# Queries and keys by half a Strassen product, and attention in one order written by hand

## The chip, the cores and the metric

The kernel runs on one core of a Trainium2 chip. The metric is the device time in microseconds (us) of one execution, the median of several. The engines of a core are TensorE (PE; PEld are its weight loads), VectorE (DVE), ScalarE (ACT) and GpSimd (POOL); SyncE (SP) issues the DMAs. Each engine takes its instructions in the order in which they stand in its own list, and waits there for the semaphores of others. Matmuls write PSUM banks of 128 x 512 float32; everything else lives in SBUF.

## The reference

Two layers on x of 1024 rows and 1024 columns: dilated attention, then a state-space layer (S5). The change touches the attention:

```python
proj = h @ w_in                       # h: 1024 x 1024
n_qkv = 3 * N_GROUPS_A * ATTN_WIDTH   # 3 groups, 16 heads of 64
qkv = proj[..., :n_qkv].reshape(B, S, 3, N_GROUPS_A, ATTN_HEADS, HEAD_DIM)
z = proj[..., n_qkv:]
for g, (window, dilation) in enumerate(((128, 1), (512, 4), (2048, 16))):
    o, l = dilated_group_attention(qkv[:, :, 0, g], qkv[:, :, 1, g], qkv[:, :, 2, g],
                                   rel_bias, window, dilation)
    ...
wts = jax.nn.softmax(jnp.stack(lses), axis=0)
o = jnp.sum(wts[..., None] * jnp.stack(outs), axis=0)
return (o * jax.nn.silu(z)) @ w_out
```

Inside a group each query meets up to 128 + 1 keys at steps of the dilation: logits with a bias, softmax, and a weighted sum of values. The three groups' outputs are merged by their log-sum-exps, gated, and projected out.

## The kernel before

All large products are done in fp32r with a high and a low part of each operand and three products: high x high, low x high, high x low. `split` makes the parts: ACT casts the high part (L88, for queries with a factor at L91), and DVE, or POOL for the attention's weights, subtracts it from the source (L89, L92).

The stages follow one another: norm and transposition of x to h (two row halves th of 512, kept as hh and hl), the values of all heads by Strassen-Winograd products (class Quads, L431), which leaves seven sums of h in SBUF; then the attention; then its gates and out-projection (`attn_gate`, L115 again and L966), then layer 1.

The attention runs over 8 pairs of heads and 3 groups: 24 units. A unit loads and splits a 1024 x 128 weight of queries, makes the two row halves of the queries in a PSUM bank each (`proj_half` and `proj_part`, L115: 8 blocks of the contraction x 3 products = 24 matmuls of 128x512 a bank), and `evac_q` splits a bank into qh and ql in the group's own order of rows. The same is done for the keys (`evac_k`: kh and kl). Then, for each of two halves u of the query tiles (`attn_unit`): logits into psl (L530), bias and running maximum on DVE (L536), the negated maxima nm (L542), exponentials on ACT (L547), transposes into pt (L558), their split to ph, and value products into pso (L607, or L633 for the last group), copied and added to O (L617, L618, L638). `put_ms` sends maxima and sums through DRAM (transpose ptm, L645). When a pair is complete, `merge_weights` computes the three groups' weights, and POOL multiplies each O by its weights mw, loaded back from DRAM (L748), and adds them up (L750). Between these, POOL also makes rotation tables for layer 1 (L1397 to L1402).

Two banks (psj) hold projections, two pairs of banks psl hold logits, two each are for pt and pso; q and k tiles have two buffers each, lg and ph three. The order on each engine is the Tile scheduler's: the program is written unit by unit, with projections' loads and splits and the logits put ahead by `high_priority(AHEAD)`. It thereby mixes a unit's projections with the transposes and value products of the units before. After the last pair the gates (8 heads' pairs x 2 row halves x 24 matmuls, L115) mix with the end of the attention in the same way; the last pair's merged O, its gate and its split gh are what the last part of the out-projection needs.

Of the kernel before, what the change touches and what calls it, by code (L numbers as in the profile page):

```python
# [52 lines left out]

class Ctx:
# [40 lines left out]
def load_w(c, src):  # L95

    nc = c.nc
    with c.tc.high_priority(AHEAD):
        raw = c.wraw.tile([P, KT * P], F32, tag="wraw", name="wraw")
        nc.sync.dma_start(raw, src)  # L100
        hi = c.wsp.tile([P, KT * P], F32R, tag="whi", name="whi")
        lo = c.wsp.tile([P, KT * P], F32R, tag="wlo", name="wlo")
        c.last_lo = split(c, hi, lo, raw, engine=c.w_engine).ins
    return hi, lo
# [147 lines left out]
def evac_k(c, ps, g, t0, k):  # L252

    n = ps.shape[1] // ORD[g]
    at = t0 // ORD[g]
    hi, lo = (t.rearrange("p (r l) -> p r l", r=ORD[g])[:, :, at:at + n] for t in k)
    split(c, hi, lo, ps.rearrange("p (l r) -> p r l", r=ORD[g]))


# [42 lines left out]
class Quads:  # L302
# [4 lines left out]
    def __init__(self, c):  # L307
# [8 lines left out]
        def tt(o, x, y, op):  # L316
            nc.vector.tensor_tensor(o, x, y, op=op)

        def parts(slots, t):
            hi, lo = (c.vslot(s, F32R) for s in slots)  # L320
            split(c, hi, lo, t)
            return hi, lo
# [19 lines left out]
        self.rows = [a11, a12, s4, a22, s1, s2, s3]  # L342
# [7 lines left out]
    def quad(self, raw, order, product, banks, use):  # L350
# [12 lines left out]
        def weights(i):  # L363
            with c.tc.high_priority(AHEAD):
# [13 lines left out]
                hi, lo = (c.wsp.tile([P, KT * P], F32R, tag=t, name=t)[:, 0:4 * n].rearrange("p (k x) -> p k x", k=4)  # L378
# [103 lines left out]
def load_v(c, p, g):  # L482


    nc = c.nc
    vp = c.attn.tile([P, KT, P], F32, tag="vp", name="vp", bufs=1)
    o = ORD[g]
    off = c.v_dr.offset + (g * 2 + p // 4) * S * H + p % 4 * P

    for dst, at, step in (((vp, 0, P),), ((vp[:, 0::2], 0, 1), (vp[:, 1::2], o * P, 1)), ((vp, 0, 1),))[g]:  # L490
        src = bass.AP(c.v_dr.tensor, off + at * H, [[o * H, P], [step * H, dst.shape[1]], [1, P]])
        nc.sync.dma_start(dst, src)
    vs = c.attn.tile([P, KT, 2, P], F32R, tag="vs", name="vs", bufs=1)
    if g == 2:
        split(c, vs[:, :, 0], vs[:, :, 1], vp)
    else:
        split(c, vs[:, :, :, 0:64], vs[:, :, :, 64:128], vp.rearrange("p b (h d) -> p b h d", h=2))
    return vs


# [3 lines left out]


def attn_unit(c, g, u, q, k, v, bt, ms, O):


    nc = c.nc
    qh, ql = q  # L510
    kh, kl = k
    lg = c.attn.tile([P, 2, 4, 256], F32, tag="lg", name="lg", bufs=3)
    tiles = []
    for js in ((0, 1, 2, 3),) if g == 2 else ((0, 1), (2, 3)):

        psl = c.psa.tile([P, 2, H], F32, tag="psl", name="psl")
        parts, at = [], 0
        for j in js:
            qt = u * 4 + j
            m = (7 - qt, 1 - qt % 2, 0)[g]  # L520
            start = (max(m - 1, 0) * P, qt // 2 * 256, qt * P)[g]
            w = 256 if m else 128
            tiles.append(w)
            parts.append((j, slice(at, at + w), slice(qt * P, qt * P + P), slice(start, start + w)))
            at += w
        with c.tc.high_priority(AHEAD):
            for j, o, qs, ks in parts:
                for n, (x, y) in enumerate(((qh, kl), (ql, kh), (qh, kh))):
                    for h in range(2):
                        nc.tensor.matmul(psl[:, h, o], x[HEADS[h], qs], y[HEADS[h], ks],  # L530
                                         start=j == js[0] and n == 0, stop=n == 2, skip_group_check=True)
        for j, o, _, _ in parts:
            w = tiles[j]
            for h in range(2):
                col = ms_col(g, 0, h, u * 4 + j)
                nc.vector.tensor_tensor_reduce(  # L536
                    lg[:, h, j, 0:w], psl[:, h, o], bt[:, h, 256 - w:256], scale=1.0, scalar=-3.0e38,
                    op0=ALU.add, op1=ALU.max, accum_out=ms[:, col:col + 1])
    nm = c.small.tile([P, 2, 4], F32, tag="nm", name="nm")
    at = (4 - 4 * u, 4 * u, 4 * u)[g]  # L540
    mx = ms[:, 0:16].rearrange("p (h t) -> p h t", h=2)[:, :, at:at + 4]
    nc.vector.tensor_scalar(nm, mx, -1.0, None, op0=ALU.mult)  # L542
    for h in range(2):
        for j, w in enumerate(tiles):
            col = ms_col(g, 1, h, u * 4 + j)
            b = (3 - j, j ^ 1, j)[g]
            nc.scalar.activation(lg[:, h, j, 0:w], lg[:, h, j, 0:w], AF.Exp, bias=nm[:, h, b:b + 1],  # L547
                                 accum_out=ms[:, col:col + 1])
    (pv_last if g == 2 else pv_first)(c, g, u, lg, v, O)
    if u == 1:  # L550
        put_ms(c, g, ms)


def transposed(c, lg, blocks, name):

    pt = c.pst.tile([P, H], F32, tag="pst", name=name)
    for n, (h, j, part) in enumerate(blocks):
        c.nc.tensor.transpose(pt[:, n * P:(n + 1) * P], lg[:, h, j, part * P:part * P + P], c.ident)  # L558
    return pt


def split_weights(c, pt, wd):
    t = c.attn.tile([P, 2, H], F32R, tag="ph", name="ph", bufs=3)
    hi, lo = t[:, 0], t[:, 1]
    split(c, hi[:, 0:wd], lo[:, 0:wd], pt[:, 0:wd])
    return hi, lo
# [12 lines left out]
def pv_first(c, g, u, lg, vs, O):  # L579


    nc = c.nc

    if g == 0:
        first = [(6 - 4 * u - j, j, [(j, 0), (j + 1, 1 if j < 2 or u == 0 else 0)]) for j in range(3)]
        single = [(7 - 4 * u, 0, [(0, 1)])]
        if u == 0:
            single.append((3, 3, [(3, 0)]))
        banks = [first[:2], first[2:] + single]
    else:  # L590
        banks = [[(4 * u + j, j, [(j, 0), (j + 1, 0)]) for j in (0, 2)],
                 [(4 * u + 1 + j, j, [(j, 1)]) for j in (0, 2)]]
    for h in range(2):
        po = c.pso.tile([P, H], F32, tag="pso", name="pso")
        jobs = []
        for bank in banks:
            blocks = [(h, j, part) for _, _, parts in bank for j, part in parts]
            wd = P * len(blocks)
            hi, lo = split_weights(c, transposed(c, lg, blocks, "pt"), wd)
            at = 0  # L600
            for kb, col, parts in bank:
                n = P * len(parts)
                for x in (hi, lo):
                    jobs.append((po[:, col * P:col * P + n], vs[:, kb, h], x[:, at:at + n]))
                at += n
        for n, (o, l, r) in enumerate(jobs):
            nc.tensor.matmul(o, l, r, start=n == 0, stop=n == len(jobs) - 1, skip_group_check=True)  # L607
        out = out_tile(c, g, O)

        rows = HEADS[h]  # L610
# [6 lines left out]
        nc.scalar.copy(dst, fr[0])  # L617
        nc.vector.tensor_tensor(dst, dst, fr[1], op=ALU.add)  # L618


def pv_last(c, g, u, lg, vs, O):


# [78 lines left out]
def attn_pair(c, p, w_in, h):  # L702
# [3 lines left out]
    for g in range(3):  # L706
# [17 lines left out]
        if g == 1:  # L724
            run_merge(c)
# [1061 lines left out]
```

## Time and profile before

| what | us |
|---|---|
| median of 3 runs | 1662.56 (1661.94 to 1662.82) |
| span of the profiled execution | 1660.9 |
| the attention's eight pairs | about 332 to 1097 in the span |
| PE / DVE / ACT / POOL busy in the span | 1640.8 / 1025.7 / 710.2 / 460.7 |

Only the span of the profiled execution is known of it; it lies 1.7 us below the median of the runs. Rows of grouped instructions give the line, engine, operation, output <- inputs, shapes, count, then busy time and mean ns of one, then the engine's idle time before them and what ended it. Rows of windows give for each engine the busy time in a stretch and (after x) the instructions, then PE's granted clock, the share of DMA time and GB/s. Rows of the chain of waits give start, length and what ran.

### The profile page before, as it was taken

Reading aid. Unit: us, or ns where it says so; the run is one execution under the profiler, and the core shown is the slowest. Engines: PE = TensorE matmul, PEld = TensorE weight load, DVE = VectorE, ACT = ScalarE, POOL = GpSimd, SP = SyncE. Lnnn points to the kernel's source line nnn. Section 1 sums busy time; section 2 is a strip of 40 time slices with the busy share of each in tenths; the row PEclk is TensorE's granted clock in tenths of the full one; section 3 lists DMA queues with packets and bytes.
Section 4 is the critical chain, followed back from the end, with each engine's and each line's share of the span. In section 5 each row is a group of like instructions: output and inputs, shape, how many; then the busy total and the mean of one; then the engine's idle time right before and its main releaser. Section 6 shows DMA issues by size and latency. Waiting matters only on the chain.

```text
span 1660.9 us, 26398 instructions
## 1 busy us (share of the span) xinstructions
PE 1640.8 (99%) x9750; PEld 1390.4 (84%) x9750; DVE 1025.7 (62%) x2515; ACT 710.2 (43%) x1732; POOL 460.7 (28%) x301
## 2 busy tenths in 40 slices
PE   8999999999999999999999999999999999999998
PEld 6889999988888888888888888888888888878886
DVE  7799999725455454545545454557564799855533
ACT  5232233326556464655645465565353132334411
POOL 1000010131342522424253252503320455422121
PEclk9999999999999999999999999999999999999999
DMA  6223455441232323324243332516336888654532
GB/s 249 70 46 108 154 172 175 139 142 55 69 103 71 104 81 92 93 64 108 71 111 87 92 106 60 150 52 192 118 121 201 245 247 242 214 190 159 159 110 87
DMA packets 176858, 212.21 MB, mean 128 GB/s; under 512 B 37443, under 2 KB 133462, under 8 KB 176728
## 3 DMA queue, kind: packets, MB, share of 16 engines
q1 hardware_dynamic: 176728, 210.52, 42.6%
q8 instruction: 77, 1.26, 0.3%
q14 instruction: 53, 0.43, 0.1%
HBM read 153.51 MB, written 56.96 MB: 127 GB/s over the span
## 4 chain that ended last, share of the span: by engine, by line
PE 76%; DVE 5%; POOL 2%; issue 1%; DMA 1%; ACT 0%; SPq 0%; DVEq 0%; POOLq 0%; ACTq 0%
PE psj L115 44%; PE pso L966 9%; PE psq L431 5%; PE psl L530 5%; PE pso L607 4%; PE pt L558 4%; PE pso L633 1%; PE psb L115 1%; DVE T L1488 1%; DVE T L1493 1%; POOL fz L923 0%; PE pv L1481 0%; PE pst L132 0%; POOL Y L1512 0%; DMA fz<-on_dr 0%
## 5 line engine op out<-in xcount | busy, mean ns | idle before, releaser
L115 PE MATMUL psj<-hh,whi 128*128 128x512 f32 x896 | 358.3, 400 | 0.0
L115 PE MATMUL psj<-hl,whi 128*128 128x512 f32 x896 | 354.9, 396 | 0.0
L115 PE MATMUL psj<-hh,wlo 128*128 128x512 f32 x896 | 349.8, 400 | 0.0
L89 POOL TENSOR_TENSOR wlo<-wraw,whi 128x1024 fp32r<-128x1024 f32 x48 | 115.3, 2401 | 396.1 <-ACT whi L88 396.1
L115 PEld LDWEIGHTS psj<-hh,whi 128*128 128x128 f32 x896 | 168.9, 188 | 36.7
L115 PEld LDWEIGHTS psj<-hl,whi 128*128 128x128 f32 x896 | 168.8, 188 | 36.1
L115 PEld LDWEIGHTS psj<-hh,wlo 128*128 128x128 f32 x896 | 168.5, 188 | 36.4
L547 ACT ACTIVATE lg<-lg,nm 128x128 f32<-128x128 f32 (+1 forms) x384 | 168.2, 443 | 37.0 <-DVE nm L542 37.0
L536 DVE CUSTOM_DVE_ANT_0 lg<-psl,T 128x128 f32<-128x128 f32 (+1 forms) x384 | 110.6, 347 | 88.8 <-PE psl L530 88.8
L88 ACT CAST whi<-wraw 128x1024 fp32r<-128x1024 f32 x80 | 83.6, 1046 | 114.7 <-PE psj L115 74.8
L431 PE MATMUL psq<-whi,v 128*128 128x256 f32 x640 | 115.4, 280 | 0.0
L89 DVE TENSOR_TENSOR kl<-psj,kh 128x512 fp32r<-128x512 f32 x48 | 33.2, 692 | 119.5 <-ACT kh L88 119.0
L89 DVE TENSOR_TENSOR ph<-pt,ph 128x512 fp32r<-128x512 f32 (+2 forms) x160 | 96.8, 622 | 15.5 <-ACT ph L88 13.5
L115 PE MATMUL psj<-h1h,whi 128*128 128x512 f32 (+1 forms) x272 | 103.9, 387 | 0.0
L115 PE MATMUL psj<-h1l,whi 128*128 128x512 f32 (+1 forms) x272 | 102.5, 381 | 0.2 <-DVE h1l L89 0.2
L88 ACT CAST ph<-pt 128x512 fp32r<-128x512 f32 (+2 forms) x160 | 81.6, 530 | 47.2 <-PE pt L558 46.3
L431 PEld LDWEIGHTS psq<-whi,v 128*128 128x128 f32 x640 | 98.4, 188 | 1.0 <-ACT whi L88 0.6
L431 PE MATMUL psq<-wlo,v 128*128 128x256 f32 x320 | 89.1, 279 | 0.0
L607 PE MATMUL pso<-ph,vs 128*128 128x256 f32 (+1 forms) x544 | 86.5, 284 | 0.0
L1344 POOL TENSOR_TENSOR Ks<-Ks,O 128x16 f32<-128x16 f32 x8 | 4.1, 508 | 288.7 <-ACT Ks L1342 275.0
L558 PE MATMUL pt<-identr,lg 128*128 128x128 f32 x560 | 82.0, 276 | 0.0
L607 PEld LDWEIGHTS pso<-ph,vs 128*128 128x128 f32 x544 | 73.5, 189 | 6.5
(282 smaller groups left out, 3632.2 us busy)
## 6 DMA issues: line engine op xcount, KB each, us to landing
wraw<-in_w_in_dram SPq DMA_DIRECT2D x56, 512.0 KB
v<-in_w_v_dram SPq DMA_DIRECT2D x24, 512.0 KB
mw<-wt_dr SPq DMA_DIRECT2D x48, 256.0 KB
vp<-v_dr SPq DMA_DIRECT2D x16, 512.0 KB
wraw<-in_ssm_w_in_dram SPq DMA_DIRECT2D x16, 512.0 KB
v_dr<-v SPq DMA_DIRECT2D x30, 256.0 KB
rot_dr<-rt SPq DMA_DIRECT2D x48, 128.0 KB
ca_dr<-ca SPq DMA_DIRECT2D x32, 144.0 KB
```

What stands on the lines that cost most here:

```text
L88: c.last_hi = nc.scalar.copy(hi, src).ins
L89: return (engine or nc.vector).tensor_tensor(lo, src, f32(hi), op=ALU.subtract)
L115: nc.tensor.matmul(ps, w[n == 2][:, k * P:k * P + P], h[n == 1][:, k, :], start=first and k == 0 and m == 0, stop=m == len(order) - 1 and ...
L431: nc.tensor.matmul(o, r[x][:, k, ts], w[y][:, k, :], skip_group_check=True, start=i in (0, 4, 5) and t % 2 == k == n == 0, stop=k == 3 and ...
L530: nc.tensor.matmul(psl[:, h, o], x[HEADS[h], qs], y[HEADS[h], ks], start=j == js[0] and n == 0, stop=n == 2, skip_group_check=True)
L536: nc.vector.tensor_tensor_reduce(lg[:, h, j, 0:w], psl[:, h, o], bt[:, h, 256 - w:256], scale=1.0, scalar=-3.0e38, op0=ALU.add, op1=ALU.ma ...
L547: nc.scalar.activation(lg[:, h, j, 0:w], lg[:, h, j, 0:w], AF.Exp, bias=nm[:, h, b:b + 1], accum_out=ms[:, col:col + 1])
L558: c.nc.tensor.transpose(pt[:, n * P:(n + 1) * P], lg[:, h, j, part * P:part * P + P], c.ident)
L607: nc.tensor.matmul(o, l, r, start=n == 0, stop=n == len(jobs) - 1, skip_group_check=True)
L633: nc.tensor.matmul(po[:, n].rearrange("p h q -> p (h q)"), vs[:, kb, x], w[:, s], start=n == 0 and m == 0, stop=n == 1 and m == 2, skip_gr ...
L966: nc.tensor.matmul(ps, x[:, k, ts], y[:, k, cols], start=n == m == 0, stop=n == KT - 1 and m == len(todo) - 1)
L1488: nc.vector.tensor_tensor_scan(T1[:, j], c.rho[:, g:g + 1].to_broadcast([P, P]), T1[:, j], 0.0, op0=ALU.mult, op1=ALU.add)
```

## The change

*Fewer matmuls.* The contraction of 1024 has 8 blocks of 128. For half of them queries and keys of a unit are computed together, as a 2 x 2 block product of the row halves of h with the two weights, in the seven products of Strassen-Winograd (`form`, with the sums of h that the values' stage left, c.forms); for the other half straight (`straight`). A form is 2 blocks x 3 products = 6 matmuls of 128x512, a straight product 4 x 3 = 12: 42 + 48 = 90 a unit at L562 instead of 96.

*Sums in two banks.* Bank X takes products 0, 2, 4, 6 and 8 and accumulates through all of them; after 0, 2 and 4 ACT copies its state to SBUF (p1, u2, u3), read in the group's order. Bank Y is opened three times, and DVE adds it, read in the same order, to these copies (L583, four times). One half of the queries and both halves of the keys are then split from the sums in SBUF, the other half of the queries from X.

*Weights.* Instead of two splits of 128x1024 a unit makes five of 128x512 and one of 128x256 (w1 to w6), with four subtractions of 128x256 on POOL between them (L546).

*One order.* The units are objects, and `attn_units` runs 26 steps. In step m unit m is projected, unit m - 1 does logits, exponentials and its first transposes and value products, and unit m - 2 the rest, its `put_ms` and the merge, which is in two parts, in two successive steps, with mw in pieces of 128x512. `Program` chains what each call issues on PE, ACT, DVE and POOL behind what the call before issued there; SP's DMAs are left to the scheduler. The queries and keys and the logits now have one buffer (of one and of two banks), X and Y one bank each.

*Around it.* The values' stage does its additions and splits of 128x2048 as two halves; some tables move to other pools; rotation tables are loaded in pieces; the maxima of a merge and its weights are made in two functions.

```diff
+    def block(self, ps, w, a, rows, ks, start, stop):
+        order = [(b, x, y) for b in range(2) for x, y in ((0, 0), (1, 0), (0, 1))]
+        for m, (b, x, y) in enumerate(order):
+            c.nc.tensor.matmul(ps, w[:, y, a, b * P:b * P + P], rows[x][:, ks + b, :], start=start and m == 0,
+                                      stop=stop and m == 5, skip_group_check=True)
+
+    def form(self, ps, i, w, a, start=False, stop=True):
+        self.block(ps, w, a, self.c.forms[i], 0, start, stop)
+
+    def straight(self, ps, w, th, start=False, stop=True):
+        self.block(ps, w, 0, self.c.h[th], 2, start, False)
+        self.block(ps, w, 1, self.c.h[th], 6, False, stop)
...
+    def copy(self, name):
+        t = self.c.slot(name, tag="a").rearrange("p (r l) -> p r l", r=ORD[self.g])
+        self.c.nc.scalar.copy(t, self.order(self.X, name == "p1"))
+        return t
+
+    def add(self, t):
+        self.c.nc.vector.tensor_tensor(t, t, self.order(self.Y, t is self.p1), op=ALU.add)
...
+        elif n == 1:
+            self.w6 = self.halves(k[:, 1, 0].unsqueeze(1), "w6", c.attn)
+            for o, x, y in ((q[:, 0, 0], k[:, 0, 0], q[:, 0, 0]), (k[:, 0, 0], k[:, 1, 0], k[:, 0, 0]),
+                            (k[:, 1, 0], k[:, 1, 0], q[:, 0, 0]), (q[:, 1, 0], q[:, 1, 0], k[:, 1, 0])):
+                self.engine.tensor_tensor(o, x, y, op=ALU.subtract)
...
+        for i in self.c.nc.cur_bb.bb.instructions[before:]:
+            if i.engine in IN_ORDER:
+                self.last[i.engine] = i
...
+        run((cur, "product", 0), (two, "split_weights", 0, 1), (cur, "sums", 0))
+        if m:
+            run((cur, "weights", 5))
...
+                step(merge_weights, c, c.merge)
+            step(merge, c, c.merge, c.outputs[c.merge], two.g)
...
+        run((two, "exps", 1, 1), (cur, "product", 1), (two, "PV", 0, 1), (two, "T", 1, 0), (two, "store", 0, 1),
+            (two, "split_weights", 1, 0), (one, "logits", 0))
+        run((cur, "product", 2), (cur, "sums", 2), (cur, "product", 3), (cur, "sums", 3),
+            (two, "PV", 1, 0), (two, "T", 1, 1), (two, "store", 1, 0), (two, "split_weights", 1, 1), (one, "logits", 1),
+            (cur, "product", 4), (cur, "sums", 4), (one, "exps", 0, 0), (cur, "product", 5), (cur, "sums", 5),
+            (two, "PV", 1, 1))
...
+        run((nxt, "weights", 0), (nxt, "weights", 1))
+        run((one, "logits", 2), (one, "exps", 0, 1), (cur, "product", 6), (nxt, "weights", 2), (nxt, "weights", 3),
+            (cur, "product", 7), (cur, "sums", 7), (one, "logits", 3), (one, "T", 0, 0), (one, "split_weights", 0, 0),
+            (cur, "qk", 0), (cur, "qk", 2), (cur, "product", 8), (cur, "qk", 1), (nxt, "weights", 4), (one, "exps", 1, 0),
+            (cur, "product", 9), (cur, "sums", 9), (one, "PV", 0, 0), (one, "T", 0, 1), (cur, "qk", 3), (one, "store", 0, 0))
...
-        c.psj = pool("psj", bufs=2, space=PSUM)
+    c.psa, c.psx, c.psy = c.ps("psa", 1), c.ps("psx", 1), c.ps("psy", 1)
```

Two places of the engines' lists. The first is DVE's list where a unit's queries and keys come out of the banks, before: the parts ql and kl stand wherever the scheduler found room, here among a merge's weights (L680 to L683, cm) and ahead of a unit's maxima (L536), and all read a bank (psj).

```order
L680 TENSOR_TENSOR cm_1543<-cm_1541 64x32
L681 TENSOR_TENSOR cm_1543<-cm_1543,cm_1541 64x32
L682 RECIPROCAL cm_1543<-cm_1543 64x32
L92 SCALAR_TENSOR_TENSOR ql<-psj,qh 128x4x128
L683 SCALAR_TENSOR_TENSOR cm_1542<-cm_1542,cm_1543 64x96
L536 ISA lg,ms<-psl,T 128x256
L536 ISA ms 128x1
```

And now, in the order of the hand-written step: ql of the sum p1 and kl of the sum u2 (both in SBUF), then ql of X, then nm, the addition of Y to u3, and kl of u3.

```order
L692 ISA ms 128x1
L105 TENSOR_TENSOR ph<-pt,ph 128x512
L105 TENSOR_TENSOR ph<-pt,ph 128x256
L108 SCALAR_TENSOR_TENSOR ql<-p_6382,qh 128x8x64
L105 TENSOR_TENSOR kl<-u_6480,kh 128x8x64
L108 SCALAR_TENSOR_TENSOR ql<-x,qh 128x8x64
L703 TENSOR_SCALAR nm<-ms 128x8
L583 TENSOR_TENSOR u_6539<-u_6539,y 128x512
L105 TENSOR_TENSOR kl<-u_6539,kh 128x8x64
L783 TENSOR_TENSOR O_6740<-O_6740,pso 64x2x2x128
```

The instruction that frees X (ql<-x) stands behind two parts that read SBUF alone, and nm behind it.

The second place is PE's list at the end of the attention, where gates (L115 before, L130 now) lie between the last unit's transposes and value products. Before:

```order
L633 MATMUL pso<-ph,vs 128x256 x5
L645 MATMUL ptm<-identr,ms 32x128
L115 MATMUL psj<-hl_112,whi 128x512
L115 MATMUL psj<-hh_111,wlo 128x512 x8
L115 MATMUL psj<-hh_109,whi 128x512
L115 MATMUL psj<-hl_110,whi 128x512
```

Now:

```order
L130 MATMUL psj<-hh_111,wlo 128x512 x8
L763 MATMUL pso<-ph,vs 128x256 x6
L714 MATMUL pt<-identr,lg 128x128 x4
L763 MATMUL pso<-ph,vs 128x256 x6
L714 MATMUL pt<-identr,lg 128x128 x4
L763 MATMUL pso<-ph,vs 128x256 x6
L790 MATMUL ptm<-identr,ms 32x128
L130 MATMUL psj<-hh_111,whi 128x512
```

The last transposes and value products stand side by side now, all of them ahead of ptm, with gates only behind; 72 matmuls of the gates follow ptm up to the first of the out-projection, where 105 did. Before, six value products still came 22 gate matmuls later.

More of the change, by code (lines that the diff above doesn't have):

```diff
@@ L479, in v_phase @@
         q.values(a, ch)
[L482 to L498, printed above, removed]
@@ L501, in ms_col @@
 def ms_col(g, n, h, qt):
     return (n * 16 + h * 8 + 7 - qt, n * 16 + h * 8 + (qt ^ 1), n * 16 + h * 8 + qt)[g]
[L506 to L551, printed above, removed]
@@ L554, in transposed @@
[L554 to L566, printed above, removed]
 def out_tile(c, g, O):
@@ L1409, in bview @@
+    store(part, out)
+    if part:
+        store(2, tmp)
 def bview(ap, n):
```

483 lines of the change are left out of this document (340 added, 143 removed).

## The prediction

> **What bounds the kernel now.** I read the page's busy shares first, then the table of windows over the attention, then the chain of waits inside one period of it, then the grouped instructions, and last the chain behind the attention.
>
> ```profile
> PE 1640.8 (99%) x9750; PEld 1390.4 (84%) x9750; DVE 1025.7 (62%) x2515; ACT 710.2 (43%) x1732; POOL 460.7 (28%) x301
> PE   8999999999999999999999999999999999999998
> PE psj L115 44%; PE pso L966 9%; PE psq L431 5%; PE psl L530 5%; PE pso L607 4%; PE pt L558 4%; PE pso L633 1%; PE psb L115 1%; DVE T L1488 1%; DVE T L1493 1%; POOL fz L923 0%; PE pv L1481 0%; PE pst L132 0%; POOL Y L1512 0%; DMA fz<-on_dr 0%
> ```
>
> TensorE is busy in every slice, and the projections (L115) are 44% of the chain. The change touches 332 to 1097 us, the eight pairs. The windows are that stage, two periods of one pair, and the end of the value phase.
>
> ```profile
> 332.00:1097.00 765.00, 765.00 (x4656) 635.89 (x4655) 382.50 (x1199) 406.16 (x1173) 267.94 (x141) 1.00 0.33 92
> 453.00:550.00 97.00, 97.00 (x598) 80.82 (x597) 49.60 (x158) 52.61 (x153) 34.23 (x19) 1.00 0.31 88
> 744.20:841.30 97.10, 97.10 (x599) 80.87 (x598) 50.10 (x158) 52.61 (x153) 34.38 (x19) 1.00 0.32 87
> 160.00:240.00 80.00, 80.00 (x710) 78.36 (x709) 73.32 (x138) 20.19 (x29) 2.52 (x4) 1.00 0.48 150
> ```
>
> One pair takes 97.1 us, a unit (one group of one pair) 32.4, and PE is busy in all of it at full clock (column PEclk, 1.00). DVE has 50 of 97 us, ACT 53, POOL 34: nothing but PE's own matmuls sets the period, so a matmul removed is worth its full pitch as long as PE finds the next one ready. The pitch comes from the chain:
>
> ```profile
> 540.84 4.17 PE psj L115 x18
> 547.00 6.98 PE psj L115 x30
> 576.23 1.18 PE pso L607 x9
> 577.42 0.90 PE pt L558 x8
> ```
>
> 6.98/30 = 0.233 us for a 128x512 matmul, 4.17/18 = 0.232; I take 0.2325. (The groups' mean of 400 ns counts overlap.)
>
> **The change, part by part.** *Projections.* Before, a unit has 2 weights x 2 row halves x 8 blocks x 3 products = 96 matmuls. After, 7 forms x 2 blocks x 3 = 42, and 4 straight products x 4 blocks x 3 = 48: 90. Over 24 units 144 fewer, all on the path: 144 x 0.2325 = **-33.5 us**. Logits, transposes and value products keep their number.
>
> *Work put beside it.* Durations of the same or the nearest kinds:
>
> ```profile
> L89 POOL TENSOR_TENSOR wlo<-wraw,whi 128x1024 fp32r<-128x1024 f32 x47 | 112.9, 2401 | 394.4 <-ACT whi L88 394.4
> L1402 POOL TENSOR_TENSOR rt<-rt,rtmp 128x512 f32<-128x512 f32 x16 | 20.8, 1303 | 1.3
> L748 POOL TENSOR_TENSOR O<-O,mw 128x1024 f32<-128x1024 f32 x21 | 50.3, 2395 | 68.8 <-DMA mw<-wt_dr 68.3 <-DVE ph L89 0.4
> L88 ACT CAST whi<-wraw 128x1024 fp32r<-128x1024 f32 x49 | 51.3, 1047 | 85.4 <-PE psj L115 47.2 <-issue 35.4 <-PE psq L431 2.8
> L88 ACT CAST kh<-psj 128x512 fp32r<-128x512 f32 x47 | 27.0, 575 | 6.2 <-PE psj L115 6.2
> L91 ACT ACTIVATE qh<-psj 128x512 fp32r<-128x512 f32 x48 | 28.3, 590 | 13.4 <-PE psj L115 13.4
> L92 DVE SCALAR_TENSOR_TENSOR ql<-psj,qh 128x512 fp32r<-128x512 f32 x48 | 32.7, 680 | 68.1 <-ACT qh L91 68.0
> L618 DVE TENSOR_TENSOR O<-O,pso 64x512 f32<-64x512 f32 x61 | 42.1, 691 | 25.4 <-ACT O L617 24.4
> L88 ACT CAST ph<-pt 128x512 fp32r<-128x512 f32 x106 | 59.6, 583 | 16.4 <-PE pt L558 15.7
> L89 DVE TENSOR_TENSOR ph<-pt,ph 128x512 fp32r<-128x512 f32 x106 | 71.2, 689 | 9.5 <-ACT ph L88 8.2
> L542 DVE TENSOR_SCALAR nm<-ms 128x8 f32<-128x8 f32 x46 | 17.0, 370 | 1.0
> ```
>
> A unit gains 3 ACT copies of a bank (0.58 each by kh) and 4 DVE adds (0.69 by L618). Its casts of weights, 2 of 1024 columns, become 5 of 512 and 1 of 256: about 0.55 x 5 + 0.3 (halves and a quarter of 1.05, rounded up) against 2.1. So ACT gets 3 x (1.74 + 0.95) = 8 us more per pair, DVE 8.3. POOL's parts become 5 of 1.3 (by L1402), one of 0.65 and 4 subtractions of 0.65 (half of it), 9.7 against 4.8 a unit: 15 us more per pair. With a pair at 93 us they stand at ACT 61, DVE 58, POOL 49. As sums all three fit, at nothing. What can cost is the order: before, the scheduler let PE draw on two projection banks and on units in different stages; now each engine follows one list, X and Y are one bank each, and any wait is everybody's.
>
> *The bank X* is the tightest hand-over in a step. Its last product is followed on PE by 12 matmuls into Y (2.8 us), value products and transposes (up to 1.18 and 0.90): 4.4 to 4.9 us until the next unit's first product wants X. In that time ACT casts qh (0.59), and DVE makes ql (0.68), queued behind two parts that read only SBUF, ql of the sum p1 and kl of the sum u2 (0.68 and 0.69), and behind parts of ph. Undisturbed about 2.5 us are left. With POOL in the way they are not:
>
> ```profile
> 574.93 4.85 POOL L750 TENSOR_TENSOR O<-O,O 128x1024 f32<-128x1024 f32 x2
> 578.07 1.75 DVE L542 TENSOR_SCALAR nm<-ms 128x8 f32<-128x8 f32 x1
> L92 DVE SCALAR_TENSOR_TENSOR y0b<-zg,y0b x8: 686/1781/1822, 1496.1 to 1563.0; 128x512 fp32r<-128x512 f32 x8
> 1540.69 1.40 POOL L1606 TENSOR_TENSOR zg<-zg,yg 128x512 f32<-128x512 f32 x1 [11.06 <-DMA zg<-z_dr]
> 1540.84 1.80 DVE L92 SCALAR_TENSOR_TENSOR y0b<-zg,y0b 128x512 fp32r<-128x512 f32 x1
> ```
>
> A little nm, 0.37 in the mean, took 1.75 us and ended with POOL's second addition; the split of y0b, with both inputs in SBUF, took 1.8 beside a POOL instruction and 0.69 alone. So each of the SBUF-only parts can lose about 1.1 us, if POOL is at work when it starts. [...]
>
> POOL is busy about half of a step, two such parts precede ql, and the slack covers two collisions: 0 us in most steps, up to 1 in some. *The transposes* have a hand-over of the same kind (ph: 0.58 on ACT, 0.69 on DVE, then the value products), with a run of 18 or 12 matmuls or logits over it nearly everywhere, and about 4.2 us over the last of a step. Bounds for the steady part: 0 (all hidden) and 24 x 2 us = 48 (X late by two collisions beyond the slack in each step). I take the end near 0, since the rows' sums leave 2.5 us: 24 x 0.17 = **+4**.
>
> *Start and value phase.* Its additions and splits of 128x2048 are issued as halves, so DVE pays a second instruction's fixed time: 73.3 of 80 us are busy in that window while PE is full. I bound it by 0 and 3 us; with the first step, which has no transposes or logits to lie between: **+2**.
>
> *The end of the attention.*
>
> ```profile
> 1128.16 0.11 PE ptm L645
> 1133.50 0.61 PE pso L633 x5
> 1172.69 2.41 POOL O L764
> 1175.13 1.24 DVE O L767
> 1176.39 0.63 ACT gh L88
> 1177.06 17.45 PE pso L966 x75
> ```
>
> From the last transpose of maxima (ptm) to the last pair's gh it takes 48.9 us, on DVE and POOL; PE fills this with gates and out-projection, and waits only at its end. In the new order 72 gate matmuls instead of 105 stand behind ptm: 33 x 0.2325 = 7.7 us less cover. Against it, the last value products now stand ahead of ptm and not 5.4 us behind it, so the DVE work begins earlier, and the gap is 2.3 to 7.7 us. Ahead of it two groups of transposes are each followed at once by the value products that need them, after 0.58 + 0.69 us on ACT and DVE: 2.5 in all. Bounds 0 (the gates' share of DVE's queue is done earlier, and gh comes earlier by as much) and 10; I take the middle: **+5**.
>
> Sum against the profiled execution: 1660.9 - 33.5 + 4 + 2 + 5 = 1638.4 us of span. The median, 1662.56, is 1.7 above the span, so **1640 us**.
>
> **Rivals.** *All hidden.* PE dense through loop and tail: 1662.6 - 33.5 = 1629. For it speaks that DVE, ACT and POOL have over a third of the time free; against it the single banks and the 33 gate matmuls.
>
> *Half eaten.* Each step loses about 0.6 us at X or at ph: 24 x 0.6 = 14 in the place of the 4, so 1650, up to 1659 with the tail's upper end.
>
> *No change* is the same with 1.1 us a step: 33.5 = 24 x 1.1 + 7.
>
> *Slower: ACT held by POOL.* In the new order ACT's third cast of weights waits for POOL's subtractions (1.3 + 0.65 + 4 x 0.65 = 4.5 us of POOL after the first cast), and POOL, in one list now, does the merges ahead of them, which wait for mw from DRAM: 68.3 us in 21 instructions before, 3.3 each. Behind that cast stand ACT's casts of the logits' exponentials, of ph and of X, and PE stops at all three. It decides from 1.15 us a step; at 2 us it is +48 - 33.5 + 7, so 1684. Against it: a merge falls in two of three steps, in the first third of a step, and the cast in the last third; some 10 us lie between.
>
> **How the numbers follow.** A difference under 0.2% (3.3 us) can't be told from none. The forecast, 1632 to 1650, has 0.50; all hidden (below 1632) 0.20; half eaten (1650 to 1659) 0.11; within 3.3 us 0.05; slower 0.14. Faster is then 0.81. The range from 1624 to 1664 leaves out most of the slower case and little else.
>
> **What would show it.** A pair's period of 93 to 94 us; the pitch still 0.2325 over 2160 projection matmuls; POOL 49 us of a period; PE's idle time put to DVE ql (X) or ph, and below 0.5 us a step; a gap of 2 to 8 us ahead of the last out-projection. A period over 97, or idle time behind ACT's casts that ends with POOL, would make the prediction wrong; so would a PE clock below 1.00 in the loop.

## The result

The changed kernel takes 1684.47 us (median; 1683.15 to 1691.34) against 1662.25 (1661.79 to 1662.82) before: 1.0144 times as long, 95% interval 1.0124 to 1.0163. It is slower by 22 us where 22 us less were forecast. Beside the runs below the kernel before took 1661.2 to 1661.7 us (medians), so that times of different runs can be set side by side. Its profiled execution spans 1683.5 us. The page's busy shares and the chain's shares by engine, after, and below them the same shares of the chain before:

```profile
PE 1624.6 (97%) x9606; PEld 1373.6 (82%) x9606; DVE 1126.8 (67%) x2635; ACT 772.1 (46%) x1904; POOL 601.0 (36%) x507
PE 42%; DVE 16%; POOL 15%; issue 12%; DMA 8%; ACT 5%; SPq 1%; POOLq 0%; DVEq 0%; ACTq 0%
PE 76%; DVE 5%; POOL 2%; issue 1%; DMA 1%; ACT 0%; SPq 0%; DVEq 0%; POOLq 0%; ACTq 0%
```

The chain that ended last was 76% PE, and is 42% now, with DVE and POOL at 31%.

Two pairs of the loop, each from one last transpose of maxima to the third after it, in the table of windows after:

```profile
501.10:601.50 100.40, 95.85 (x583) 79.32 (x581) 62.62 (x170) 60.17 (x174) 54.86 (x47) 0.98 0.30 88
601.50:699.60 98.10, 94.42 (x581) 78.11 (x580) 61.26 (x169) 60.15 (x174) 51.88 (x45) 1.00 0.29 85
```

A pair takes 98.1 to 100.4 us; 97.1 less the pitch of its 18 matmuls fewer would be 92.9. ACT (60), DVE (62) and POOL (52 to 55) have about the busy time of the forecast, so no engine is the bound by its sum. PE waits:

```profile
PE x L562 <- DVE ql L108: 15.3, 15, 1.7
PE pso L763 <- ACT ph L104: 8.3, 9, 1.0
PE pso L763 <- DVE ph L105: 3.3, 10, 0.3
PE pso L1170 <- DVE wol L105: 3.2, 1, 3.2
```

(The view of PE's waits: total us, times, longest.) Such a wait costs more than its idle time: in the profile a matmul of 128x512 lasts 0.39 us while the next one starts after 0.2325, so idle time counts from a later moment than the one at which the next could have started. Counted from start to start, less the usual pitch, the loop has about 36.6 us of waits (17.7 at X, 15.7 at ph) and the end of the attention 4.5; the split moves by a few us with what is taken as the usual pitch.

Where the time went can be laid out by three landmarks: the end of the values' products, the first product of the out-projection, the end.

```profile
L431 PE MATMUL psq<-whi,v x640: 276/276/388, 128.5 to 331.6; 128*128 128x256 f32 x160
L966 PE MATMUL pso<-woh,gh x128: 388/394/502, 1153.2 to 1247.1; 128*128 128x512 f32 x128
```

```profile
L440 PE MATMUL psq<-whi,v x640: 274/279/388, 124.3 to 334.4; 128*128 128x256 f32 x160
L1170 PE MATMUL pso<-woh,gh x128: 388/392/398, 1171.1 to 1266.9; 128*128 128x512 f32 x128
```

(First before, then after; min/median/max ns, first and last start.) Up to the attention: +2.8 us. From there to the out-projection: 821.6 before, 836.7 after, +15.1; since 33.5 us of matmuls are gone, 48.6 came in. Behind it: +4.7. The 48.6 are the 36.6 and 4.5 of waits and three stretches of 3.4 us in which PE ran at half its clock (the third column from the right is the granted clock):

```profile
516.90:520.30 3.40, 3.40 (x9) 2.63 (x9) 1.49 (x4) 3.40 (x13) 0.00 (x0) 0.50 0.29 117
981.10:984.50 3.40, 3.40 (x23) 3.07 (x22) 2.87 (x5) 3.13 (x11) 1.08 (x1) 0.50 0.25 77
1151.80:1155.20 3.40, 3.12 (x11) 2.56 (x11) 1.69 (x5) 1.54 (x6) 0.00 (x0) 0.50 0.10 22
```

Each follows waits of PE and costs 1.7 us, 5.1 together; some 2.4 us of the 48.6 are not located.

What makes X late shows in the chain of waits over one step after:

```profile
502.50 1.44 POOL O L944
...
504.87 2.95 POOL w L105 x2
509.41 0.75 POOL wraw L546
...
510.18 0.03 ACT w L104
...
510.71 0.59 ACT ph L104
...
511.32 1.02 DVE ph L105 x2
512.35 1.70 DVE ql L108
514.04 1.68 DVE kl L105
515.72 0.61 DVE ql L108
...
516.38 2.52 PE x L562 x6
```

POOL ends a merge (L944), makes two low parts of weights, then the four subtractions; ACT's cast of w3 (the fourth of weights in a step, behind w1, w6 and w2) has waited for the third of them, and ph, behind it on ACT, starts at 510.71. DVE then makes ph, ql of p1, kl of u2 and at last ql of X. Two of these take 1.7 us. Meanwhile POOL, through with the fourth subtraction, makes the low parts of w2 and w3, and that of w4 behind them, by its timeline:

```profile
510.94 2.56 POOL L105 TENSOR_TENSOR w<-wraw,w 128x512 fp32r<-128x512 f32 x2
513.69 1.49 POOL L105 TENSOR_TENSOR w<-wraw,w 128x512 fp32r<-128x512 f32 x1 [0.19 <-ACT w L104]
```

The grouped instructions over the attention say the same of all steps:

```profile
L104 ACT CAST w<-wraw 128x512 fp32r<-128x512 f32 x115 | 71.1, 618 | 59.4 <-POOL wraw L546 58.2 <-DMA wraw<-in_w_in_dram 1.2
L105 DVE TENSOR_TENSOR kl<-u,kh 128x512 fp32r<-128x512 f32 x48 | 58.1, 1210 | 42.5 <-ACT kh L104 42.5
L108 DVE SCALAR_TENSOR_TENSOR ql<-p,qh 128x512 fp32r<-128x512 f32 x24 | 32.0, 1333 | 0.0
L108 DVE SCALAR_TENSOR_TENSOR ql<-x,qh 128x512 fp32r<-128x512 f32 x24 | 16.3, 677 | 0.0
```

And ACT's view of waits how long the cast is held:

```profile
ACT w L104 <- POOL wraw L546: 58.2, 23, 3.7
```

ACT waits 58 us for POOL at this cast, 2.5 us in the mean of 23 steps and up to 3.7. kl and ql from SBUF take 1.2 and 1.3 us in the mean, ql from the bank 0.68. (Of the two kl of a step only that of u2 is slow, up to 1.8 us; that of u3 takes 0.69.) So two suspects stand side by side: **the wait** (ACT held at a cast by POOL's subtractions, all of ACT's and so of DVE's work late) and **the meeting** (DVE's parts with both inputs in SBUF blocked by POOL's). The runs below take them apart.

### The profile page after: what moved, and what is told of

It reads as the page before. It is cut to its first block, busy times and chain, and to the rows that moved or that the text cites. A ratio compares the mean times of both kernels' runs of the same rounds, so it can differ in the third digit from the quotient of the medians.

```text
span 1683.5 us, 26823 instructions
## 1 busy us (share of the span) xinstructions
PE 1624.6 (97%) x9606; PEld 1373.6 (82%) x9606; DVE 1126.8 (67%) x2635; ACT 772.1 (46%) x1904; POOL 601.0 (36%) x507
## 4 chain that ended last, share of the span: by engine, by line
PE 42%; DVE 16%; POOL 15%; issue 12%; DMA 8%; ACT 5%; SPq 1%; POOLq 0%; DVEq 0%; ACTq 0%
PE psq L440 10%; PE pso L1170 10%; PE psj L130 10%; POOL w L105 4%; PE y L562 3%; POOL wraw L546 3%; DVE kl L105 2%; PE x L562 2%; DVE ql L108 2%; PE psv L298 2%; DVE ph L105 2%; DMA mw<-wt_dr 2%; ACT lg L708 2%; DVE T L1696 2%; POOL O L943 1%
## 5 line engine op out<-in xcount | busy, mean ns | idle before, releaser
L105 POOL TENSOR_TENSOR w<-wraw,w 128x512 fp32r<-128x512 f32 x138 | 185.4, 1359 | 298.2 <-ACT w L104 297.9
L562 PE MATMUL y<-hh,w 128*128 128x512 f32 x672 | 225.9, 394 | 0.0
L562 PE MATMUL x<-hh,w 128*128 128x512 f32 x384 | 139.3, 413 | 15.3 <-DVE ql L108 15.3
L562 PEld LDWEIGHTS y<-hh,w 128*128 128x128 f32 x672 | 126.8, 189 | 29.0
L562 PE MATMUL y<-hl,w 128*128 128x512 f32 x336 | 131.9, 392 | 0.0
L583 DVE TENSOR_TENSOR u<-u,y 128x512 f32<-128x512 f32 x72 | 49.2, 683 | 105.5 <-PE y L562 105.5
L104 ACT CAST w<-wraw 128x512 fp32r<-128x512 f32 x144 | 81.5, 582 | 62.5 <-POOL wraw L546 58.2
L130 PE MATMUL psj<-h1h,whi 128*128 128x512 f32 (+1 forms) x272 | 104.2, 388 | 1.6 <-ACT h1h L104 1.0
L130 PE MATMUL psj<-h1l,whi 128*128 128x512 f32 (+1 forms) x272 | 102.5, 381 | 0.2 <-DVE h1l L105 0.2
L562 PEld LDWEIGHTS x<-hh,w 128*128 128x128 f32 x384 | 72.5, 189 | 35.4 <-DVE ql L108 19.0
L105 DVE TENSOR_TENSOR kl<-u,kh 128x512 fp32r<-128x512 f32 x48 | 58.1, 1210 | 42.5 <-ACT kh L104 42.5
L1197 POOL TENSOR_TENSOR xr<-xr,y 128x512 f32<-128x512 f32 x30 | 38.1, 1293 | 130.6 <-DVE y L1196 91.9
```

The source lines that it names most:

```text
L104: c.last_hi = nc.scalar.copy(hi, src).ins
L105: return (engine or nc.vector).tensor_tensor(lo, src, f32(hi), op=ALU.subtract)
L130: nc.tensor.matmul(ps, w[n == 2][:, k * P:k * P + P], h[n == 1][:, k, :], start=first and k == 0 and m == 0, stop=m == len(order) - 1 and ...
L562: c.nc.tensor.matmul(ps, w[:, y, a, b * P:b * P + P], rows[x][:, ks + b, :], start=start and m == 0, stop=stop and m == 5, skip_group_chec ...
L583: self.c.nc.vector.tensor_tensor(t, t, self.order(self.Y, t is self.p1), op=ALU.add)
L1197: nc.gpsimd.tensor_tensor(x[:, ns], x[:, ns], y, op=ALU.add)
```

## The experiments

**Free X first.** The queue ahead of ql of X is turned round, and the tiles of queries and keys are allocated at what is now the first of them.

```diff
-        if n == 0:
+        if n == 1:
             self.q, self.k = ([c.attn.tile([P, S], F32R, tag=x + y, name=x + y, bufs=1) for y in "hl"] for x in "qk")
...
-            (cur, "qk", 0), (cur, "qk", 2), (cur, "product", 8), (cur, "qk", 1), (nxt, "weights", 4), (one, "exps", 1, 0),
+            (cur, "product", 8), (cur, "qk", 1), (cur, "qk", 0), (cur, "qk", 2), (nxt, "weights", 4), (one, "exps", 1, 0),
```

> One edit to the changed kernel: the part of the queries that lies in bank X is split (ACT qh, DVE ql) ahead of the three parts that are split from sums in SBUF, so X is free before DVE takes those up. Theory Q (the two parts with both inputs in SBUF, held up by POOL, stand in DVE's list ahead of the one that frees X): the waits of x for DVE ql, 17.7 us in 15 places with the drain of PE, and the half-clock stretch behind one of them go; -15 to -20 us, about 1666. Rival W (ACT is late as a whole, since its cast of weights waits for POOL's subtractions): X is freed by ACT and DVE as late as before; -5 us at most, above 1678.

1674.27 us, 1.0077 times before (1.0062 to 1.0092): 10 us less, between the two. PE's waits in it:

```profile
PE pso L763 <- DVE ph L105: 10.9, 22, 1.0
PE y L562 <- DVE u L583: 6.4, 10, 0.8
```

The waits at X are gone, and others stand in their place, for what DVE does behind: the addition of Y, the next ph. DVE as a whole is late; turning its queue takes away 10 of the 40 us that the next run does, and for the rest chooses who waits.

**Take ACT's casts out of the way.** The casts of w2 and w3 go behind the cast of X (the texts on record call w3's the third).

```diff
-        run((one, "logits", 2), (one, "exps", 0, 1), (cur, "product", 6), (nxt, "weights", 2), (nxt, "weights", 3),
+        run((one, "logits", 2), (one, "exps", 0, 1), (cur, "product", 6),
...
-            (cur, "qk", 0), (cur, "qk", 2), (cur, "product", 8), (cur, "qk", 1), (nxt, "weights", 4), (one, "exps", 1, 0),
+            (cur, "qk", 0), (cur, "qk", 2), (cur, "product", 8), (cur, "qk", 1), (nxt, "weights", 2), (nxt, "weights", 3), (nxt, "weights", 4), (one, "exps", 1, 0),
```

> One edit to the changed kernel: the second and third cast of the next unit's weights, the one of which waits for POOL's subtractions, stand behind the cast of bank X on ACT instead of ahead of the exponentials and of ph. Theory W: ph, qh and kh come 2.5 to 3.7 us earlier, and DVE with them; -15 to -20 us, about 1667. Theory Q: POOL's splits of weights now follow later too, so DVE's parts from SBUF meet fewer of them, but they still stand ahead of ql of X; -5 to -15.

1644.32 us, 0.9894 times before (0.9877 to 0.991): 40 us less than the changed kernel, twice the most that either theory gave. A pair, in the windows, and the groups:

```profile
588.50:681.30 92.80, 92.80 (x582) 78.07 (x580) 57.18 (x169) 60.31 (x174) 51.77 (x45) 1.00 0.31 91
```

```profile
L104 ACT CAST w<-wraw 128x512 fp32r<-128x512 f32 x115 | 66.8, 626 | 0.9 <-DMA wraw<-in_w_in_dram 0.9
L105 DVE TENSOR_TENSOR kl<-u,kh 128x512 fp32r<-128x512 f32 x48 | 35.4, 737 | 40.8 <-ACT kh L104 40.7
L108 DVE SCALAR_TENSOR_TENSOR ql<-p,qh 128x512 fp32r<-128x512 f32 x24 | 18.9, 788 | 0.0
```

PE is busy in all of 92.8 us, with the same work on ACT and POOL. Both suspects went at once: ACT's wait fell from 59 us to 1, and kl and ql to 0.74 and 0.79, because POOL can make the low parts of w2 and w3 only after their casts, and these now stand behind that of X. So the written order carries the loss, but which of the two is not told yet.

**The merge's maxima later.** Once per pair PE waits for ph, and on ACT the cast of that ph stands behind a small exponential of the merge. This moves.

```diff
             if two.g == 0:
+                step(merge_maxima, c)
                 step(merge_weights, c, c.merge)
...
             if two.p < 7:
-                step(merge_maxima, c)
                 c.merge = two.p
```

> One edit to the changed kernel: a merge's maxima (cm on DVE, one small exponential on ACT) stand behind the next step's first split of ph instead of ahead of it. If this exponential, which waits for DVE's cm and so for a load from DRAM, is what holds the value products once per pair (7 x about 1.5 us with the drain), -8 to -11 us, about 1675, and one pair of half-clock windows less. If ph was late for another reason there (the transposes), no difference.

1673.49 us, 1.0073 (1.0052 to 1.0094): 11 us less, as expected. But in the run with the casts late, which left the maxima where they were, PE has no wait for ph in the loop at all. The two runs below that part the suspects tell with which it goes: without the meeting it is gone, though ACT waits as before, and with the meeting alone it is there again, 1.1 us once per pair. So by these runs it goes with a late DVE, which makes cm ahead of the exponential.

**The scheduler's order.** `Program` issues without the chain.

```diff
             for i in self.last.values():
-                es.enter_context(self.c.tc.issue_after(i))
+                pass
```

> The changed kernel without the chain of its order: the same instructions, banks, buffers and casts, but each engine's order is the Tile scheduler's. If the loss is the written order's: PE finds other work at X and at ph, and the time is 1640 to 1660. If the loss lies in the additional work and the single banks, whatever the order: 1675 or more.

1669.9 us, 1.005 (1.0035 to 1.0065): neither. The scheduler loses less than the written order did and far more than a good one. A pair takes about 97.1 us in it, of which PE is idle 1.6 us; where the other 2.6 us over 92.9 go was not located.

**One cast alone.** Only w3's, whose source the subtractions make.

```diff
-        run((one, "logits", 2), (one, "exps", 0, 1), (cur, "product", 6), (nxt, "weights", 2), (nxt, "weights", 3),
+        run((one, "logits", 2), (one, "exps", 0, 1), (cur, "product", 6), (nxt, "weights", 2),
...
-            (cur, "qk", 0), (cur, "qk", 2), (cur, "product", 8), (cur, "qk", 1), (nxt, "weights", 4), (one, "exps", 1, 0),
+            (cur, "qk", 0), (cur, "qk", 2), (cur, "product", 8), (cur, "qk", 1), (nxt, "weights", 3), (nxt, "weights", 4), (one, "exps", 1, 0),
```

> The changed kernel with only the third cast of weights (w3, the one whose source POOL's subtractions make) moved behind the cast of bank X on ACT; the second stays where it was. Theory W (ACT held at this one cast): nearly all of the 40 us that moving both gave, about 1646. If the gain came from moving POOL's splits away from DVE's parts that read SBUF, the split of w2 still lies there, and about half of it, 1664.

1651.15 us, 0.9937 (0.9922 to 0.9952): 33 of the 40 us, nearer to the wait's number. kl and ql stay slow in part (1031 and 969 ns in its groups), so it takes away all of the wait and about half of the meeting's loss on DVE. It doesn't part the two; and the half that is left costs only 6.8 us, so the price of a meeting is not in proportion to it.

**The low parts on DVE, twice.** ACT's casts stay where they were; DVE makes the low parts of w2 and w3, first right behind ql of X, then at the end of its step (the new step `low`).

```diff
+    def low(self):
+        for w, src in self.pending:
+            self.c.last_lo = self.c.nc.vector.tensor_tensor(w[:, 1], src, f32(w[:, 0]), op=ALU.subtract).ins
...
-            (cur, "qk", 0), (cur, "qk", 2), (cur, "product", 8), (cur, "qk", 1), (nxt, "weights", 4), (one, "exps", 1, 0),
+            (cur, "qk", 0), (cur, "qk", 2), (cur, "product", 8), (cur, "qk", 1), (nxt, "low"), (nxt, "weights", 4), (one, "exps", 1, 0),
```

> The changed kernel's order, ACT's wait at the cast of w3 included, but the low parts of w2 and w3 are made by DVE behind ql of X instead of by POOL at once: no POOL instruction beside ql of p1 and kl of u2, which then take 0.7 us each instead of 1.3 and 1.2. Theory W alone: X comes as late as before, since ph, qh and kh start late; 1680 or more. Theory L (the meeting of DVE and POOL eats the slack): the waits for ql go, -15 to -20 us, about 1666; the wait for ph once per pair stays in both.

> As the run with the low parts of w2 and w3 on DVE, but these two stand at the end of DVE's step, behind kl of u3, so that neither nm nor the addition of Y waits for them. ACT's wait at the third cast stays, no POOL instruction stands beside ql of p1 and kl of u2. Theory W alone: 1675 or more. Theory L, or both together eating one slack: X, Y and the second ph come in time, only the wait for ph once per pair stays, 1660 to 1668.

1685.77 us (1.0145, 1.0127 to 1.0163) and 1701.58 (1.0236, 1.0221 to 1.0251). PE's waits in the two:

```profile
PE pso L776 <- DVE ph L105: 11.2, 23, 0.8
PE pso L776 <- ACT ph L104: 9.2, 9, 1.1
PE y L575 <- DVE u L596: 8.9, 13, 0.9
```

```profile
PE y L575 <- DVE w L547: 34.6, 22, 2.2
```

In the first, kl and ql take 0.71 and 0.69 us and nothing waits at X, but the two additional parts on DVE make the addition of Y and ph late instead. In the second the next unit's second product waits for the low part of w2 itself. Both times lie in theory W's range, but not for its reason, since X comes in time. Both runs moved load to the engine that was late already; of wait and meeting they tell nothing clean.

**The wait without the meeting.** The low parts stay on POOL, but behind that of w4, whose cast follows X's; ACT's casts stay.

```diff
+            self.c.last_lo = self.engine.tensor_tensor(w[:, 1], src, f32(w[:, 0]), op=ALU.subtract).ins
...
-        run((one, "logits", 2), (one, "exps", 0, 1), (cur, "product", 6), (nxt, "weights", 2), (nxt, "weights", 3),
+        run((one, "logits", 2), (one, "exps", 0, 1), (cur, "product", 6), (nxt, "high", 2), (nxt, "high", 3),
...
-            (cur, "qk", 0), (cur, "qk", 2), (cur, "product", 8), (cur, "qk", 1), (nxt, "weights", 4), (one, "exps", 1, 0),
+            (cur, "qk", 0), (cur, "qk", 2), (cur, "product", 8), (cur, "qk", 1), (nxt, "weights", 4), (nxt, "low"), (one, "exps", 1, 0),
```

> The changed kernel with ACT's casts where they stand, the wait of the third for POOL's subtractions included, but POOL's low parts of w2 and w3 issued behind that of w4, whose cast follows that of bank X: no POOL instruction stands beside ql of p1 and kl of u2, and DVE gets nothing to do in addition. What this takes from 1684 is the meeting's share, what is left above 1644 the wait's. Wait alone decides: 1675 or more. Meeting alone decides: 1650 or less. Both eat the same slack: X comes in time (kl and ql 0.7 us), the wait for ph once per pair stays (about 9 us), 1655 to 1668.

1655.98 us, 0.9971 (0.9961 to 0.998): inside the last of the three ranges. Its groups:

```profile
L105 DVE TENSOR_TENSOR kl<-u,kh 128x512 fp32r<-128x512 f32 x48 | 35.5, 740 | 42.6 <-ACT kh L104 42.5
L541 ACT CAST w<-wraw 128x512 fp32r<-128x512 f32 x46 | 28.2, 613 | 58.5 <-POOL wraw L559 55.1 <-PE x L575 3.4
L108 DVE SCALAR_TENSOR_TENSOR ql<-p,qh 128x512 fp32r<-128x512 f32 x24 | 16.7, 696 | 0.0
```

PE's largest wait:

```profile
PE pso L776 <- DVE ph L105: 7.8, 22, 0.6
```

ACT waits as long as in the changed kernel (55 us for POOL), DVE meets nothing at these parts, and PE waits for ph, in nearly every step and at most 0.6 us; for ql of X it doesn't wait at all. The time is as expected, the wait not: that for ph once per pair, which was to stay, is gone from the loop, and small ones in all steps stand in its place. Taken away in this order, the meeting is worth 1684.5 - 1656.0 = 28.5 us, and the wait, with the 1.2 us of the two casts themselves ahead of ph, 1656.0 - 1644.3 = 11.7.

**The meeting without the wait.** Casts late, and POOL makes the two low parts of DVE once more into a scratch tile.

```diff
         split(c, hi, lo, src, None if n else 0.125)
+        if n != 3:
+            t = c.slot("junk", tag="b").rearrange("p (r l) -> p r l", r=ORD[g])
+            c.nc.gpsimd.tensor_tensor(t, src, f32(hi), op=ALU.subtract)
...
```

> Both casts late (1644 as such), and POOL makes ql of p1 and kl of u2 a second time into a scratch tile, starting with the same casts as DVE's two parts: the meeting of the engines is back, ACT's wait is not. Theory L alone: DVE's two parts take 1.2 to 1.8 us each again and X is late, +15 to +20, about 1662. Theory W alone, or both needed: the 2.5 us of slack at X hold it, within 4 us of 1644.

1671.61 us, 1.0054 (1.0037 to 1.0071): 27.3 us more than with both gone, at the meeting's own price above, and more than expected. The groups, and one of PE's waits:

```profile
L105 DVE TENSOR_TENSOR kl<-u,kh 128x512 fp32r<-128x512 f32 x48 | 63.9, 1331 | 42.7 <-ACT kh L104 42.7
L640 POOL TENSOR_TENSOR junk<-u,kh 128x512 f32<-128x512 f32 x24 | 42.0, 1751 | 0.1
L108 DVE SCALAR_TENSOR_TENSOR ql<-p,qh 128x512 fp32r<-128x512 f32 x24 | 33.0, 1376 | 0.0
```

```profile
PE pso L766 <- ACT ph L104: 9.0, 9, 1.1
```

The two parts are slow again, and POOL's are too (1751 ns for the work that takes 1.3 alone). X holds this time, against what was expected; PE waits for ph instead (17.4 us in its view of waits, 9.0 of them put to ACT's part). The mean granted clock of its profiled execution was 0.993, as in that of the run with both gone. It is no pure test, since POOL also has 3 us more to do in each step. But 11.7 for the wait and 27.3 or 28.5 for the meeting make 39 to 40, and both together cost 40.2.

**The subtractions on DVE.** The wait is to become short, not to move.

```diff
-                self.engine.tensor_tensor(o, x, y, op=ALU.subtract)
+                c.nc.vector.tensor_tensor(o, x, y, op=ALU.subtract)
```

> The changed kernel's order with the four subtractions of 128x256 on DVE instead of POOL: ACT's third cast stays ahead of ph, but waits for DVE (4 x 0.4 us) and no longer for 4 x 0.74 us behind POOL's two low parts and merges. Theory W (the length of that wait on ACT is what matters, not the place of the cast): the 58 us of ACT's waiting fall to under 30, and the time to 1650 to 1665. If the place alone matters: 1675 or more.

1741.32 us, 1.0479 (1.0459 to 1.0498), the opposite of what was expected. ACT's wait at the cast did not become short: 55.7 us in all, for DVE now; so the run does not tell its length from its place.

```profile
L546 DVE TENSOR_TENSOR wraw<-wraw 128x256 f32<-128x256 f32 x92 | 73.8, 802 | 28.9 <-POOL w L105 23.7 <-DMA cm<-ms_dr 1.2
```

```profile
PE psl L686 <- DVE ms L692: 58.4, 16, 4.9
```

(A row of the groups, and one of PE's waits.) The subtractions overwrite what POOL's first low parts read, so DVE now waits for POOL, and the maxima of the logits stand behind it in DVE's list; PE stops at the one buffer of logits, up to 4.9 us at a time.

**What a matmul is worth.** Casts late, and one form of each unit issued twice.

```diff
             self.form(self.Y, 4, self.w4, 0, start=True)
+            self.form(self.Y, 4, self.w4, 0, start=True)
...
```

> Both casts late, as before in the run that gave 1644, and one form of 6 matmuls of every unit issued twice into bank Y (the second overwrites the first): 144 matmuls of 128x512 more, with the same values. If PE alone sets the time now and the pitch is 0.2325 us: +33.5, about 1678. If a hand-over still binds in places, less.

1674.88 us, 30.6 more than without, 3 less than forecast; the profiled spans differ by 32.7. A pair in its windows:

```profile
502.20:599.20 97.00, 97.00 (x601) 81.48 (x599) 57.69 (x170) 60.30 (x174) 51.49 (x46) 1.00 0.31 90
```

97.0 - 92.8 = 4.2 us for 18 matmuls, 0.233 each: the pitch of the forecast.

**A version that beats both.** Casts late, maxima late, and in the last step each group of transposes ahead of the value products of the one before.

```diff
+        if m == 25:
+            run((two, "exps", 1, 1), (two, "T", 1, 0), (two, "split_weights", 1, 0), (two, "PV", 0, 1), (two, "T", 1, 1),
+                (two, "store", 0, 1), (two, "split_weights", 1, 1), (two, "PV", 1, 0), (two, "store", 1, 0), (two, "PV", 1, 1))
...
```

> Both casts late, the merge's maxima late, and in the last step transposes issued one stage ahead of their value products. The runs so far leave 2.6 us of waits in the loop and 4.5 behind it, and one half-clock window of 1.7 us: 1644 less up to 6, about 1639; no difference if the maxima no longer matter and the last gh sets the end of the attention anyway.

1639.17 us, 0.9868 (0.9851 to 0.9886). A pair takes 92.6 us:

```profile
587.40:680.00 92.60, 92.60 (x582) 77.99 (x581) 57.39 (x170) 60.29 (x174) 52.19 (x46) 1.00 0.32 93
```

```profile
PE pso L1179 <- DVE wol L105: 4.3, 1, 4.3
```

(A window, and the largest of PE's waits.) Of what the change touches, a wait of 4.3 us in the out-projection is the largest that is left.

## Why the prediction was wrong

*The matmuls* (-33.5): right. 144 are gone, and where nothing hides it a pair falls from 97.1 to 92.8, 8 x 4.3 = 34 us.

*The work as sums* (ACT 61, DVE 58, POOL 49 of 93): 60, 57 to 59 and 52 to 54 where the order leaves it alone, 60, 61 to 63 and 52 to 55 in the changed kernel, where DVE's surplus is in its parts from SBUF: kl takes 1.21 us in the mean there for 0.74, ql of p1 1.33 for 0.79.

*The steady part* (+4): this is the step that failed. The forecast set the meetings of DVE and POOL down as chance: POOL "busy about half of a step, two such parts precede ql, and the slack covers two collisions: 0 us in most steps", and took "the end near 0" of 0 to 48. With the wait at the cast of w3, which the same sum put at nothing, it cost 40.2 us, 1.7 a step, 27 to 29 of them for the meetings. In a fixed order they are not by chance. POOL's subtractions release both sides: the third lets the cast of w3 go, and behind it on ACT ph, qh and kh, from which DVE makes its parts; and 0.8 us later, behind the fourth, POOL itself takes up its next low parts. In the step shown ql of p1 runs into that of w3 (512.20 to 513.50), and kl of u2, pushed back by it, into that of w4; the trace has the like in every step of the loop but one (kl of u2 takes 1.75 to 1.79 us in 23 of 24 steps, 0.68 in the other). The slack of 2.5 us at X did hold either loss alone: without the meeting, and without the wait, PE doesn't wait for ql of X at all. Both together exceed it. What each costs alone is paid at ph, the hand-over that the forecast took as covered by other matmuls nearly everywhere. All of this stood in the lists of ACT and POOL before the run: which instruction on the one engine releases which on two others.

*The slower rival* had the place of the wait (a cast of weights behind POOL's subtractions, w3's), and by luck the number, 1684, but not the larger part of the cause. By itself that wait is worth 11.7 us, 0.5 a step, under its own point of 1.15 from which it decides, and the change would have been faster with it (1656). What was written against it, that some 10 us lie between the merge and the cast, missed the point: in the step shown the merge ends at 504.9 and the cast could have begun at 506.5, and in steps without a merge, as near 574 us, ACT is held there too (2.1 us), by the low parts and subtractions alone.

*The toll of a meeting*, 1.1 us for a part, was rightly read from the rows, and what the forecast let the slack cover was the answer: 24 x 0.94 us for kl of u2 and 24 x 0.64 for ql, against the run where they meet nothing, make 38 us of DVE's time, all in the one stretch of a step that has a deadline.

*Start and values* (+2): 2.8. Of the halves' fixed time the rows show little: two additions of 128x1024 take 2.42 us, one of 128x2048 took 2.29. *The end* (+5): 4.5 us of waits and 1.7 of half clock as far as the out-projection, and 4.7 behind it, where the forecast had nothing. Of its two parts the wait at the last transposes came (2.1 us for 2.5); the gap at gh did not, and the largest single wait was at the low parts of the out-projection's weights (wol, 3.2 us).

With the one step mended the sum nearly holds: 1644 for an order without wait and meeting, against the 1640 forecast, with 4.9 us that the forecast lacked (512.5 against 507.6 from the first product of the out-projection to the end). The 1639 has two more edits which the forecast did not have; that it comes closer is luck.

## What to carry to other kernels

In an order written by hand, follow each instruction that others wait for to what it releases on every other engine: two instructions that are released by neighbours in one list meet in nearly every turn of the loop (here in 23 of 24), and their collision is no matter of shares of busy time. Put work for the next turn behind the work of this one that has a deadline, above all where its source comes from a slower engine (POOL took 0.74 us for a subtraction of 128x256, DVE 0.42 with nothing beside it); here that alone was worth 40 us. Turning a late engine's queue round, or giving it the blocked work, mostly moves the wait (here 1674 us for the one, 1686 and 1702 for the other, against 1684).

## What the runs showed of the hardware

A short wait of PE can cost more than itself. Its timeline of the changed kernel ahead of the first two of the half-clock stretches shown above (idle time before an instruction in brackets):

```profile
516.38 0.50 PE L562 MATMUL x<-hh,w 128*128 128x512 f32 x1 [1.68 <-DVE ql L108]
979.39 0.38 PE L763 MATMUL pso<-ph,vs 128*128 128x256 f32 x1 [0.97 <-ACT ph L104]
980.11 1.62 PE L763 MATMUL pso<-ph,vs 128*128 128x256 f32 x9 [0.34 <-DVE ph L105]
```

After 1.7 us of idleness six matmuls took 2.52 us, 0.42 each instead of 0.2325. After a wait of the same length at another place the clock stayed whole (5.10 us with PE busy in 3.42):

```profile
712.90:718.00 5.10, 3.42 (x17) 2.61 (x16) 3.25 (x5) 3.09 (x11) 0.75 (x1) 1.00 0.31 103
```

In this trace the half-clock stretches behind the start of the attention begin at 516.88, 981.09, 1151.76, 1482.85 and 1680.82 us. The first three last 3.413 us each, the fourth 6.827, and the fifth runs into the end of the span. 136, 50, 97 and 58 times 3.413 us lie between the starts, whole numbers to within 0.02. What makes one wait count and another not stays open: in the 3.41 us up to 714.85, a point of the same grid, PE is busy for 1.73 us and idle for one whole wait of 1.68, and in the 3.41 us up to 516.88 as well; behind the first the granted clock was 1.00, behind the second 0.50. One gap of 1.7 us, and two of 0.97 and 0.34 us close together ahead of 981, stood ahead of such a stretch, once each.

POOL pays for the meeting as well, in two of three steps: the low parts of w2, w3 and w4 take 4.68 us at 544.58, 1.56 each, beside ql of p1 and kl of u2, and that of w4 1.49 at 513.69; at 574.95 and 577.91 all three keep to 1.30. The doubled kl takes 1.75, and the low parts of w2 and w3 take 1.30 in the run where they meet nothing.
